# Modulation sections g1, sh2, sc2 and g2 of a hybrid mLSTM/attention block: from float32 products on TensorE to sums on GpSimd during attention

## The chip, the cores and the metric

The kernel runs on one core of one Trainium2 chip. The metric is the device time of one execution in microseconds (us). A profile is one more execution, recorded instruction by instruction; its times are counted from its first instruction. The engines are named PE (TensorE), DVE (VectorE), ACT (ScalarE), POOL (GpSimd) and SP (SyncE, which here issues most of the DMAs). PEld is TensorE's loading of weights.

## The reference, cut to what matters

```python
silu_c = jax.nn.silu(c)                               # [1, 1024]
mod = (silu_c @ w_mod[l] + b_mod[l])[:, None, :]      # [1024] @ [1024, 6144]
sh1, sc1, g1, sh2, sc2, g2 = jnp.split(mod, 6, axis=-1)
h = rmsnorm(x, norm1_g[l]) * (1.0 + sc1) + sh1
y, yc = token_mix(h, hc, w_in[l], ...)                # projections, mLSTM, attention, merge
x = x + g1 * y
x = x + g2 * swiglu(rmsnorm(x, norm2_g[l]) * (1.0 + sc2) + sh2, w_ffn_gate[l], w_ffn_up[l], w_ffn_down[l])
```

One layer, 1024 tokens, width 1024, a context of 256 tokens, 8 query heads and 2 key/value heads of 128 in attention. The modulation is a vector times a matrix of 1024 by 6144. Its first two sections (sh1, sc1) are wanted at once; the other four (g1, sh2, sc2, g2, each 1024 columns) only after attention.

## The kernel before, in words

All large products are float32 products by three TensorE products of halves (`mm3`: high by high, high by low, low by high; each operand is split by `split`, ACT writing the high half and DVE or POOL the low one, line 99). The order is: first modulation, norm, transposes; 25 units of projections; mLSTM heads; first half of the merge; attention; second half of the merge; output projection by halves of the tokens and quarters of the columns; feed-forward; down.

Big tiles of 4 KB a partition ("slots", tile name `s`) are given out and taken back in a ring; PSUM banks come from four tags (X, K, Y, Z). The program text sets what is computed; a scheduler behind it decides in which order the instructions stand on each engine, and each engine then works through its own list in that order, waiting on semaphores. SP's list of DMAs is in order too.

The four later sections are computed by `modulation_rest(ps, i)` in eight blocks of 512 columns, each called once between other stages: blocks 0 and 1 (g1) after projection units 14 and 15, blocks 4 to 7 (sh2, sc2) in the second half of the merge after column tiles 1, 2, 4 and 5, blocks 2 and 3 (g2) in the output projection after quarters 1 and 2. A block (`mod_block`, tile `macc`) loads four slots of 512 KB of w_mod and makes eight plain float32 products whose weights are the silu(c) columns, on four column tiles of TensorE side by side (line 300); DVE copies the four partial rows out of PSUM (line 304); then either one product with a selector sums them to a row (tile `mg`, line 344) which goes to DRAM with its bias, or four small ones sum them and put channels on partitions (tile `mch`, line 312).

Attention (`attention`, a generator) goes through 16 tiles: two key/value groups of eight tiles of 128 tokens, each tile four heads; a step is one head. A step makes scores of the next head (tile `sc`), transposes the probabilities of this one (tile `pt`), and makes a quarter of the product of probabilities and values of the tile before (`attn_values`, bank `av`, of which there is one). In the second quarter the inverse sums of rows (tile `dg`, set to zero by POOL at line 1100) are transposed and copied by DVE (tile `rrow`, line 1073), and POOL spreads them over all partitions by four `partition_broadcast` (tile `rs`, line 1076):

```python
            rows = pool.tile([P, P], F32, name="rrow", tag="rrow", bufs=1)
            nc.vector.tensor_copy(rows, rb[:, 0:P])
            self.rs = pool.tile([P, 512], F32, name="rs", tag="rs", bufs=1)
            for h in range(4):
                nc.gpsimd.partition_broadcast(self.rs[:, h * P:(h + 1) * P], rows[32 * h:32 * h + 1, :])
```

In the fourth quarter DVE multiplies `av` by `rs` into `yaf` (line 1080), which frees the bank. Besides these broadcasts POOL has in attention the zeroing of `dg` and, once, five low halves of the values of the second group (tile `vv`).

Of the kernel before, what the change touches and what calls it, by code (L numbers as in the profile page):

```python
# [17 lines left out]
P = 128  # L18
# [19 lines left out]
class Slots:  # L38
    """Tiles of 4 KB a partition, given out and taken back by hand."""
# [22 lines left out]
    def drop(self, pool):  # L62
        """Gives out no more tiles of a pool."""
        self.gone.append(pool)
        self.free = [x for x in self.free if x[0] is not pool]


class Carve:
    """Small tiles out of slots."""
# [18 lines left out]
class Block:  # L88
# [12 lines left out]
    def mm3(self, out, lhs, rhs, first, last):  # L101
        """out (+)= lhs^T rhs, with lhs and rhs as (hi, lo)."""
        nc = self.nc
        nc.tensor.matmul(out, lhsT=lhs[0], rhs=rhs[0], start=first, stop=False)  # L104
        nc.tensor.matmul(out, lhsT=lhs[0], rhs=rhs[1], start=False, stop=False)  # L105
        nc.tensor.matmul(out, lhsT=lhs[1], rhs=rhs[0], start=False, stop=last)  # L106

    def rstd(self, pool, ss, n, name):
        """(ss / n + eps) ** -0.5 for a small tile of sums of squares."""
# [14 lines left out]
    def load_s(self, slots, w, k0, nk, c0, n, scale=None, lo_eng=None):  # L124
        """Columns c0..c0+n of nk row blocks of w, as (hi, lo) slots [P, nk, n]."""
# [10 lines left out]
    # ------------------------------------------------------------------ constants  # L136
    def constants(self):
# [6 lines left out]
        # selectors over the four column tiles of the modulation products  # L144
# [3 lines left out]
        # additive masks of the two scan directions: key on partitions, query along the row  # L148
# [5 lines left out]
    def channel_params(self, ps):  # L154
        """Per-channel vectors, channel on partitions."""
# [19 lines left out]
        # silu of the conditioning vectors, one column per stream, padded to a column tile  # L175
# [8 lines left out]
    # ------------------------------------------------------------------ products by seven  # L184
    # C = A B by 2 x 2 blocks, A the transposed weights, B the rows by channel:
    #   P1 = A11 B11   P2 = A12 B21   P3 = S4 B22   P4 = A22 T4   P5 = S1 T1   P6 = S2 T2   P7 = S3 T3
    #   S1 = A21 + A22   S2 = S1 - A11   S3 = A11 - A21   S4 = A12 - S2
    #   T1 = B12 - B11   T2 = B22 - T1   T3 = B22 - B12   T4 = B21 - T2
    #   U2 = P1 + P6   U3 = U2 + P7   C11 = P1 + P2   C12 = U2 + P5 + P3   C21 = U3 + P4   C22 = U3 + P5
    RIGHT = {1: "11", 2: "21", 3: "22", 4: "4", 5: "1", 6: "2", 7: "3"}  # L190

    def grow(self, *names):
        """Room for two more channel blocks of each right operand."""
        for name in names:
            self.B.setdefault(name, []).append([self.slots.get([P, 2, 512], F32R) for i in range(2)])
# [9 lines left out]
    def t_stage(self, w, col):  # L205
        """A pair of column tiles of w, by halves of its rows."""
# [5 lines left out]
    def t_own(self, u):  # L212
        """A11 and A12."""
# [12 lines left out]
    def t_sums(self, u):  # L226
        """S1 over A21, S2 over A11, S4 over A12; S3 ready."""
# [13 lines left out]
    def t_rest(self, u, i):  # L241
        """S2 and S1, or S4 and A22."""
# [13 lines left out]
    def combine(self, n, o, c11, c12, c21, c22, early=False):  # L256
        """Takes product n into the blocks of C; early: product 4 comes before 6 and 7."""
# [26 lines left out]
    # ------------------------------------------------------------------ modulation  # L284
    def mod_block(self, ps, tag, cols):
        """Four column tiles of partial sums of (silu(c), silu(c_ctx)) @ w_mod at two runs of 256 columns."""
# [20 lines left out]
    def mod_channels(self, rows, ps, tag, n):  # L307
        """Sums the partial rows and puts channels on partitions: [P, 4, n]."""
# [7 lines left out]
    def modulation_first(self, ps, half):  # L316
        """Scale A1 and shift B1 of both streams for channel blocks 0, 1, 4, 5 or 2, 3, 6, 7."""
# [15 lines left out]
    def modulation_rest(self, ps, i):  # L333
        """Block i of 8: g1, g2 (rows to DRAM), sh2, sc2 (channels on partitions)."""
        nc = self.nc
        bm = self.ch("b_mod")
        j0, b = (2, 5, 3, 4)[i // 2], i % 2
        c0 = j0 * D + b * 512
        rows = self.mod_block(ps, "X", (c0, c0 + 256))
        if i < 4:  # L340
            row = self.slots.get([P, 1024], F32)
            nc.sync.dma_start(row[0:1, 0:512], self.io["b_mod"][0:1, c0:c0 + 512])
            o = ps("Y", "mg")
            nc.tensor.matmul(o[0:2, :], lhsT=self.sel, rhs=rows[:, 0], start=True, stop=True)
            nc.vector.tensor_tensor(row[0:1, 512:1024], o[0:1, :], row[0:1, 0:512], op=ALU.add)
            nc.sync.dma_start(self.d_g[i // 2:i // 2 + 1, b * 512:(b + 1) * 512], row[0:1, 512:1024])
            self.slots.put(rows, row)
            return
        m = self.mod_channels(rows, ps, "Y", 1)[:, :, 0]
        hs = slice(4 * b, 4 * b + 4)  # L350
        if j0 == 3:
            nc.vector.tensor_tensor(self.B2[:, hs], m, bm[:, 24 + 4 * b:28 + 4 * b], op=ALU.add)
        else:
            t = self.st.tile([P, 4], F32, name="modt2", tag="modt2", bufs=2)
            nc.vector.tensor_tensor(t, m, bm[:, 32 + 4 * b:36 + 4 * b], op=ALU.add)
            nc.vector.scalar_tensor_tensor(out=self.A2[:, hs], in0=t, scalar=1.0, in1=self.ch("norm2_g")[:, hs], op0=ALU.add, op1=ALU.mult)

    # ------------------------------------------------------------------ norm, transposes
# [10 lines left out]
    def first_norm(self, rows):  # L369
        """Rows of ctx and x over their norms."""  # L370
# [9 lines left out]
    def first_turn(self, k, fc):  # L380
        """h = xhat * A + B for channel block k, channels on partitions: lat, ctx."""
# [15 lines left out]
    def first_mods(self, q):  # L397
        """Channel blocks 0, 1, 4, 5 or 2, 3, 6, 7 of h, and the right operands from them."""
# [34 lines left out]
    # ------------------------------------------------------------------ gates  # L433
    def gate_loads(self):
        """Stationary operands: (hi, lo) columns for the high part of h, (hi, 0) for its low part."""
# [14 lines left out]
    def gates(self):  # L450
        """Gates of every token: G [P, NP, 16]."""
# [23 lines left out]
    # ------------------------------------------------------------------ projections  # L475
# [3 lines left out]
    def t_unit(self, kind, col, dst):  # L479
        """256 columns of h @ w_in, transposed: the load steps and the products."""  # L480
# [64 lines left out]
    def taps(self, out, z, ch, n):  # L545
        """Five taps along a row with zeros around it, bias and silu."""
# [24 lines left out]
    def tok_unit(self, kind, cols, dst):  # L571
        """Two runs of 256 columns of h @ w_in, tokens on partitions."""
# [99 lines left out]
    def rows_of(self, dst, t, m, c):  # L672
        """Columns c..c+256 of m token tiles."""
        return dst[t * P:(t + m) * P, c:c + 256].rearrange("(t p) c -> p t c", p=P)

    # ------------------------------------------------------------------ attention operands
    def attn_tables(self):
        """Rope tables and norm gains, the scale of the scores in that of q."""
# [8 lines left out]
    def head_norm(self, z, g, junk):  # L687
        """RMS norm of two heads of a few token tiles, in place."""
# [30 lines left out]
    # ------------------------------------------------------------------ mLSTM heads  # L719
    def head_load(self, h):  # L720
        """Operands of a head, as load steps."""
# [33 lines left out]
    def head(self, pool, h, X):  # L755
        """Steps of one head; heads take turns."""
        nc, slots, ps = self.nc, self.slots, self.ps
        # keys with tokens on partitions, and q k^T of every lat tile: both directions use it
# [72 lines left out]
        # norm over the head, gain, sigmoid(o), channels on partitions  # L831
# [21 lines left out]
    def merge_load(self, hp, n):  # L853
        """Four row blocks (two heads) of 256 columns of w_pa."""
        self.wpa[hp, n] = self.load_s(self.slots, self.io["w_pa"], 4 * hp, 4, n * 256, 256, lo_eng=self.nc.vector)

    def merge_unit(self, hp, n):
        """Columns n of sigmoid(zg_m) * (ym @ w_pa), transposed: the part of two heads."""
# [26 lines left out]
    def row_rstd(self, pool, xts, nm, junk):  # L885
        """rsqrt(mean x^2 + eps) of row tiles [P, D]."""
# [6 lines left out]
    # ------------------------------------------------------------------ gate scans  # L893
    def gate_scan(self, G):
        """Per token and (direction, head, tile): a = li - F, the weights of the state and of the
        state's update, exp(-m_t), and rows of -B for the products."""
# [17 lines left out]
        # rows: (head, tile) on partitions, tokens along the row  # L914
# [19 lines left out]
        # the end values of every (head, tile) on all partitions  # L934
# [22 lines left out]
        # back to tokens on partitions  # L957
# [25 lines left out]
        # rows of -B to DRAM, to be broadcast over partitions  # L983
# [7 lines left out]
    # ------------------------------------------------------------------ attention  # L991
# [20 lines left out]
    def attn_q(self, pool, ps, g, t):  # L1012
        """q of four heads of one kv group for a token tile, transposed and split."""
# [11 lines left out]
    def attn_scores(self, pool, ps, h, qt, kt):  # L1025
        """Scores of one head and the negated row maxima."""
# [11 lines left out]
    def attn_exp(self, pool, h, sc, st, dg):  # L1038
        """exp(s - max) of one head; the inverse row sums go to a column of dg."""
# [20 lines left out]
    def attn_values(self, pool, ps, g, t, PT, vv, dg, ya, part):  # L1060
        """A quarter of p^T v for four heads of a token tile; the last one scales by the inverse sums."""
# [21 lines left out]
    def attention(self, pool, ps):  # L1083
        """A generator: the first step readies the operands, the second the first scores, then
        it takes the pools of the products and runs to the end."""
# [24 lines left out]
        ptp, ya = yield  # L1110
# [730 lines left out]
```

## Time and profile before

| what | value |
|---|---|
| median of 3 runs | 2320.58 us (2313.97 to 2321.31) |
| span of the profiled execution | 2315.2 us, 31157 instructions |
| busy PE / PEld | 2175.2 us (94%) / 1797.7 us (78%) |
| busy DVE / ACT / POOL | 1590.1 us (69%) / 995.3 us (43%) / 763.8 us (33%) |
| mean granted TensorE clock | 0.975 |
| attention, first to last broadcast of `rs` | 1106.5 to 1386.4 us |

The page gives the profiled execution by its span, and no time around it; the median of the runs lies 5.4 us above that span. A busy share is an average over stages: in attention PE is busy throughout and POOL hardly at all. PE's clock is given as a share of full speed; where it stands near 0.5 the engine runs at the lower of its two levels (1.2 of 2.4 GHz).

### The profile page before, as it was taken

Reading aid. Unit: us, or ns where it says so; the run is one execution under the profiler, and the core shown is the slowest. Engines: PE = TensorE matmul, PEld = TensorE weight load, DVE = VectorE, ACT = ScalarE, POOL = GpSimd, SP = SyncE. Lnnn points to the kernel's source line nnn. Section 1 sums busy time; section 2 is a strip of 40 time slices with the busy share of each in tenths; the row PEclk is TensorE's granted clock in tenths of the full one; section 3 lists DMA queues with packets and bytes.
Section 4 is the critical chain, followed back from the end, with each engine's and each line's share of the span. In section 5 each row is a group of like instructions: output and inputs, shape, how many; then the busy total and the mean of one; then the engine's idle time right before and its main releaser. Section 6 shows DMA issues by size and latency. Waiting matters only on the chain. (4 is left out here: it accounts for less than half of the span.)

```text
span 2315.2 us, 31157 instructions
## 1 busy us (share of the span) xinstructions
PE 2175.2 (94%) x11387; PEld 1797.7 (78%) x11387; DVE 1590.1 (69%) x2855; ACT 995.3 (43%) x1997; POOL 763.8 (33%) x619
## 2 busy tenths in 40 slices
PE   5899999999999798999999998999899999999996
PEld 2698888978887686877888886789688888876875
DVE  5666576566879785876887873365846464678997
ACT  5434434243443564643777772134523232334332
POOL 2322232312323140311001004331554444457765
PEclk8999999999999899999999999999899999999999
DMA  7132232243233922046000016661143323265421
GB/s 259 55 93 100 92 101 96 92 141 128 84 101 107 307 70 97 10 144 220 15 22 21 15 42 218 220 225 57 46 132 96 109 94 111 96 218 179 159 91 73
DMA packets 179577, 262.43 MB, mean 113 GB/s; under 512 B 13136, under 2 KB 119640, under 8 KB 179424
## 3 DMA queue, kind: packets, MB, share of 16 engines
q1 hardware_dynamic: 169504, 236.62, 30.9%
q10 hardware_dynamic: 9920, 23.82, 2.6%
q8 instruction: 90, 1.47, 0.3%
q14 instruction: 63, 0.52, 0.1%
HBM read 190.10 MB, written 70.30 MB: 112 GB/s over the span
## 5 line engine op out<-in xcount | busy, mean ns | idle before, releaser
L98 ACT ACTIVATE s<-s 128x1024 fp32r<-128x1024 f32 (+2 forms) x446 | 369.2, 851 | 684.4 <-DVE s L233 74.5
L104 PE MATMUL pr<-s,s 128*128 128x512 f32 (+1 forms) x1736 | 624.7, 361 | 19.5 <-DVE s L261 9.9
L106 PE MATMUL pr<-s,s 128*128 128x512 f32 (+1 forms) x1736 | 623.9, 360 | 7.4 <-POOL s L99 4.5
L105 PE MATMUL pr<-s,s 128*128 128x512 f32 (+1 forms) x1736 | 624.1, 360 | 7.1 <-POOL s L99 5.1
L99 POOL TENSOR_TENSOR s<-s,s 128x1024 fp32r<-128x1024 f32 (+1 forms) x199 | 407.2, 2056 | 665.1 <-ACT s L98 488.0
L99 DVE TENSOR_TENSOR s<-s,s 128x1024 fp32r<-128x1024 f32 (+2 forms) x247 | 314.6, 1280 | 133.5 <-ACT s L98 107.1
L104 PEld LDWEIGHTS pr<-s,s 128*128 128x128 f32 x1736 | 331.2, 191 | 79.2 <-ACT s L98 13.4
L106 PEld LDWEIGHTS pr<-s,s 128*128 128x128 f32 x1736 | 329.6, 190 | 62.2 <-POOL s L99 6.7
L105 PEld LDWEIGHTS pr<-s,s 128*128 128x128 f32 x1736 | 330.2, 190 | 59.9 <-POOL s L99 6.2
L104 PE MATMUL pj<-s,s 128*128 128x512 f32 (+1 forms) x696 | 250.9, 361 | 17.9 <-DVE s L1740 13.8
L105 PE MATMUL pj<-s,s 128*128 128x512 f32 (+1 forms) x696 | 248.9, 358 | 7.3 <-POOL s L99 7.3
L106 PE MATMUL pj<-s,s 128*128 128x512 f32 (+1 forms) x696 | 248.1, 356 | 1.1 <-POOL s L99 1.1
L261 DVE TENSOR_TENSOR s<-s,pr 128x512 f32<-128x512 f32 x200 | 133.1, 680 | 83.5 <-PE pr L106 78.9
L1530 DVE TENSOR_TENSOR s<-s,pr 128x512 f32<-128x512 f32 x154 | 100.1, 678 | 111.9 <-PE pr L106 55.5
L104 PEld LDWEIGHTS pj<-s,s 128*128 128x128 f32 x696 | 133.8, 192 | 49.4 <-DVE s L1740 17.9
L105 PEld LDWEIGHTS pj<-s,s 128*128 128x128 f32 x696 | 133.7, 192 | 26.2 <-POOL s L99 7.7
L106 PEld LDWEIGHTS pj<-s,s 128*128 128x128 f32 x696 | 133.7, 192 | 21.6 <-POOL s L99 1.7
L1058 DVE TENSOR_TENSOR PT<-pt,PT 128x512 fp32r<-128x512 f32 (+1 forms) x192 | 112.5, 598 | 35.0 <-ACT PT L1057 32.9
L1043 ACT ACTIVATE pr<-sc,st 128x512 f32<-128x512 f32 (+1 forms) x192 | 118.0, 622 | 33.4 <-DVE st L1035 32.9
L1540 POOL TENSOR_TENSOR s<-s,s 128x512 f32<-128x512 f32 x44 | 67.8, 1542 | 168.1 <-ACT s L98 81.8
L1057 ACT ACTIVATE PT<-pt 128x512 fp32r<-128x512 f32 (+1 forms) x192 | 94.5, 525 | 56.1 <-PE pt L1054 56.0
L1033 DVE TENSOR_REDUCE st<-sc 128x1 f32<-128x512 f32 (+1 forms) x192 | 109.4, 589 | 0.8 <-PE sc L106 0.8
(313 smaller groups left out, 3522.4 us busy)
## 6 DMA issues: line engine op xcount, KB each, us to landing
s<-in_w_in_dram SPq DMA_DIRECT2D x60, 512.0 KB, 3.8
d_act<-s SPq DMA_DIRECT2D x74, 256.0 KB, 2.1
s<-d_act SPq DMA_DIRECT2D x37, 512.0 KB, 5.3
s<-in_w_mod_dram SPq DMA_DIRECT2D x32, 512.0 KB, 6.0
s<-in_w_ffn_gate_dram SPq DMA_DIRECT2D x22, 512.0 KB, 4.3
s<-in_w_ffn_up_dram SPq DMA_DIRECT2D x22, 512.0 KB, 3.8
s<-in_w_ffn_down_dram SPq DMA_DIRECT2D x22, 512.0 KB, 5.1
s<-in_w_mod_dram SPq DMA_DIRECT2D x32, 256.0 KB, 5.1
```

Of the source, the lines that this page charges most:

```text
L98: nc.scalar.activation(hi, src, AF.Copy)
L99: (lo_eng or nc.gpsimd).tensor_tensor(lo, src, hi.bitcast(F32), op=ALU.subtract)
L104: nc.tensor.matmul(out, lhsT=lhs[0], rhs=rhs[0], start=first, stop=False)
L105: nc.tensor.matmul(out, lhsT=lhs[0], rhs=rhs[1], start=False, stop=False)
L106: nc.tensor.matmul(out, lhsT=lhs[1], rhs=rhs[0], start=False, stop=last)
L261: eng.tensor_tensor(out, a, b, op=ALU.add)
L1033: nc.vector.tensor_reduce(st[:, j:j + 1], o[:, 0:n], axis=AX.X, op=ALU.max)
L1043: nc.scalar.activation(pr[:, s0:s0 + n], sc[j][:, 0:n], AF.Exp, bias=st[:, 3:4], accum_out=st[:, 4 + j:5 + j])
L1057: nc.scalar.activation(hi, src, AF.Copy)
L1058: nc.vector.tensor_tensor(lo, src, hi.bitcast(F32), op=ALU.subtract)
L1530: nc.vector.tensor_tensor(out, a, b, op=ALU.add)
L1540: nc.gpsimd.tensor_tensor(g, g, o, op=ALU.mult)
```

## The change

`modulation_rest` becomes a generator that attention drives with one `next` after each step. It goes through the sections g1, sh2, sc2, g2, and in each through eight row blocks of w_mod: a load of 512 KB by SP (tile `wm`, two buffers), on POOL a multiplication of the 128 by 1024 block by the silu(c) column (`tensor_scalar`) and an addition into an accumulator (`tensor_tensor`), which starts as zeros with the bias in one row. Then TensorE sums the accumulator over partitions with a tile of ones: two products of 512 columns for g1 and g2, eight products of one column for sh2 and sc2. The eight calls elsewhere go, and with them 64 float32 products, their loads and the copies out of PSUM. (Comments and blank lines that the diff also removes are left out here.)

```diff
-    def modulation_rest(self, ps, i):
-        nc = self.nc
-        bm = self.ch("b_mod")
-        j0, b = (2, 5, 3, 4)[i // 2], i % 2
-        c0 = j0 * D + b * 512
-        rows = self.mod_block(ps, "X", (c0, c0 + 256))
...
+    def modulation_rest(self, pool):
+        nc, slots, ps = self.nc, self.slots, self.ps
+        sections = (2, 3, 4, 5)
+        seq = [(j0, k) for j0 in sections for k in range(KT)]
+        loaded, accs = [], {}
+        def load():
...
+            j0, k = seq[i]
+            w = pool.tile([P, D], F32, name="wm", tag="wm", bufs=2)
+            nc.sync.dma_start(w, self.io["w_mod"][k * P:(k + 1) * P, j0 * D:(j0 + 1) * D])
+            loaded.append(w)
+        def start(j0):
+            accs[j0] = slots.get([P, D], F32)
+            nc.gpsimd.memset(accs[j0], 0.0)
+            nc.sync.dma_start(accs[j0][0:1, :], self.io["b_mod"][0:1, j0 * D:(j0 + 1) * D])
+        start(sections[0])
+        load()
+        for i, (j0, k) in enumerate(seq):
+            load()
+            if k == 2 and j0 != sections[-1]:
+                start(j0 + 1)
+            acc = accs[j0]
+            nc.gpsimd.tensor_scalar(loaded[i], loaded[i], self.sc[:, k, 0:1], None, op0=ALU.mult)
+            nc.gpsimd.tensor_tensor(acc, acc, loaded[i], op=ALU.add)
+            yield
+            if k + 1 < KT:
+                continue
+            if j0 in (2, 5):
+                for b in range(2):
+                    o = ps("Y", "mg")
+                    nc.tensor.matmul(o[0:2, :], lhsT=self.ones[:, 0:2], rhs=acc[:, b * 512:(b + 1) * 512], start=True, stop=True)
+                    nc.vector.tensor_copy(acc[0:1, b * 512:(b + 1) * 512], o[0:1, :])
+                nc.sync.dma_start(self.d_g[j0 // 5:j0 // 5 + 1, :], acc[0:1, :])
+            else:
+                m = ps("Y", "mch")
+                for j in range(KT):
+                    nc.tensor.matmul(m[:, j:j + 1], lhsT=acc[:, j * P:(j + 1) * P], rhs=self.ones[:, 0:1], start=True, stop=True)
...
+            slots.put(accs.pop(j0))
+            yield
@@ attention
-        ptp, ya = yield
+        ptp, ya, side = yield
...
             pr = nxt() if nxt else None
+            next(side, None)
@@ run
-            if i in (14, 15):
-                self.modulation_rest(PS, i - 14)
...
-        attn.send((pt, yaf))
+        wm, close_wm = pool("wm")
+        attn.send((pt, yaf, self.modulation_rest(wm)))
+        close_wm()
...
-            if n in (1, 2, 4, 5):
-                self.modulation_rest(PS, 3 + n if n < 3 else 2 + n)
...
-            if not half and u in (1, 2):
-                self.modulation_rest(PS, 1 + u)
```

How the lists of the engines move is seen at two places. First POOL's list in attention, before, at the first two tiles (`ISA` without operands is a pair of instructions that sets POOL up for another set of functions, in the profile MODIFY_POOL_CONFIG; `ISA rs<-rrow` is the broadcast):

```order
L1100 MEMSET dg 128x128
L1076 ISA
L1076 ISA rs<-rrow 128x128 x4
L1100 MEMSET dg 128x128
L1076 ISA rs<-rrow 128x128 x4
```

POOL's list after the change, from the end of the second tile into the third (line numbers are those of the changed file: 352 zeroes an accumulator, 362 multiplies, 363 adds, 1102 is the broadcast):

```order
L363 TENSOR_TENSOR s_9831<-s_9831,wm 128x1024
L1102 ISA
L1102 ISA rs<-rrow 128x128 x4
L362 ISA
L362 TENSOR_SCALAR wm<-wm,sc 128x1024
L352 MEMSET s_10373 128x1024
L363 TENSOR_TENSOR s_9831<-s_9831,wm 128x1024
L362 TENSOR_SCALAR wm<-wm,sc 128x1024
L1102 ISA
L1102 ISA rs<-rrow 128x128
L363 ISA
L363 TENSOR_TENSOR s_9831<-s_9831,wm 128x1024
```

Between one broadcast and the next there now stand multiplications and additions, and an `ISA` on either side of each broadcast group; in some tiles the four broadcasts are parted as well. In attention the list before has this `ISA` twice ahead of broadcasts and twice ahead of additions; the list after has it 20 times ahead of broadcasts and 20 times ahead of multiplications or additions; of the latter the last, behind the last broadcast, is in either list.

Second, PE's list in the second half of the merge, before, between column tiles 1 and 2 (`pj` is the merge's bank):

```order
L106 MATMUL pj<-s_13410,s_9716 128x512
L300 MATMUL macc<-s_13607,sc 32x512 x2
L300 MATMUL macc<-s_13611,sc 32x512 x2
L300 MATMUL macc<-s_13615,sc 32x512 x2
L300 MATMUL macc<-s_13619,sc 32x512 x2
L104 MATMUL pj<-s_13396,s_13467 128x512
```

and the same place after the change:

```order
L106 MATMUL pj<-s_13538,s_9666 128x512
L104 MATMUL pj<-s_13524,s_13595 128x512
L105 MATMUL pj<-s_13525,s_13595 128x512
L106 MATMUL pj<-s_13524,s_13596 128x512
L104 MATMUL pj<-s_13524,s_13595 128x512
```

The eight products of the block are gone, and the next column tile follows at once.

## Rows read from the trace of the kernel before

**Rows 1.** The page, part 1: busy us, share of the span, instructions of each engine.

```profile
PE 2175.2 (94%) x11387; PEld 1797.7 (78%) x11387; DVE 1590.1 (69%) x2855; ACT 995.3 (43%) x1997; POOL 763.8 (33%) x619
```

**Rows 2.** Stretches of 40 us: length, busy us by engine, PEclk, DMA share, GB/s.

```profile
1200.00:1240.00 40.00, 40.00 (x237) 32.59 (x237) 32.18 (x83) 28.94 (x80) 4.18 (x14) 1.00 0.04 14
```

**Rows 3.** Timeline of PE: start us, busy us, line, operation, count; summing products of two blocks.

```profile
541.75 1.02 PE L344 MATMUL mg<-s,sel 128*2 128x512 f32 x2
...
1417.62 1.92 PE L300 MATMUL macc<-s,sc 128*32 128x512 f32 x16
...
1420.52 0.98 PE L312 MATMUL mch<-sel,s 128*128 128x1 f32 x8
```

**Rows 4.** Timeline, PE at three blocks; in brackets PE's idle time before and its releaser.

```profile
511.33 1.32 PE L300 MATMUL macc<-s,sc 128*32 128x512 f32 x8 [3.44 <-DMA s<-in_w_mod_dram]
...
1478.02 1.87 PE L312 MATMUL mch<-sel,s 128*128 128x1 f32 x8 [3.98 <-DVE s L304]
...
1532.06 1.38 PE L344 MATMUL mg<-s,sel 128*2 128x512 f32 x2 [2.17 <-DVE s L304]
```

**Rows 5.** Stretches of 10 us around these waits, columns as in rows 2.

```profile
500.00:510.00 10.00, 7.89 (x35) 6.13 (x33) 9.93 (x12) 5.14 (x6) 2.41 (x1) 1.00 0.83 241
510.00:520.00 10.00, 8.67 (x30) 2.82 (x30) 4.26 (x6) 2.40 (x4) 1.28 (x1) 0.83 0.69 275
...
1480.00:1490.00 10.00, 10.00 (x35) 8.01 (x36) 2.67 (x5) 1.57 (x2) 0.65 (x2) 0.76 0.71 262
...
1530.00:1540.00 10.00, 7.94 (x48) 6.72 (x49) 4.46 (x6) 2.52 (x4) 2.37 (x1) 0.83 0.83 292
```

**Rows 6.** POOL by line, 1079 to 1399: count, busy us, mean ns, idle before.

```profile
L1076 POOL PARTITION_BROADCAST rs<-rrow x64 | 20.3, 424 | 46.3 <-DVE rrow L1073 33.9 <-issue 5.9 <-DVE qt L1022 5.9
...
L99 POOL TENSOR_TENSOR s<-s,s 128x1024 fp32r<-128x1024 f32 x2 | 4.7, 2372 | 41.5 <-ACT s L98 41.5
L99 POOL TENSOR_TENSOR vv<-vr,vv 128x256 fp32r<-128x256 f32 x5 | 3.6, 732 | 12.0 <-ACT vv L98 11.9
```

**Rows 7.** POOL by line and shape, whole span, columns as in rows 6.

```profile
L799 POOL TENSOR_TENSOR qw<-s,wq 128x128 f32<-128x128 f32 x128 | 59.8, 488 | 133.7 <-PE num L807 98.1 <-ACT s L819 18.9 <-ACT sw L802 7.6
...
L783 POOL MEMSET C<- 128x516 f32 x8 | 4.1, 527 | 12.5 <-PE num L807 6.9 <-PE pr L106 5.5
...
L152 POOL TENSOR_SCALAR_AFFINE_SELECT mask<-mask 128x128 f32<-128x128 f32 x1 | 0.3, 293 | 0.0
```

**Rows 8.** Timeline of POOL at the broadcasts of tiles 0 and 8.

```profile
1088.64 2.39 POOL L99 TENSOR_TENSOR s<-s,s 128x1024 fp32r<-128x1024 f32 x1 [6.58 <-ACT s L98]
1100.34 0.21 POOL L1100 MEMSET dg<- 128x128 f32 x1 [9.32 <-PE pt L1071]
1106.48 1.29 POOL L1076 PARTITION_BROADCAST rs<-rrow  x4 [5.93 <-issue]
...
1255.64 0.20 POOL L1100 MEMSET dg<- 128x128 f32 x1 [2.52 <-PE pt L1071]
1261.74 1.29 POOL L1076 PARTITION_BROADCAST rs<-rrow  x4 [5.90 <-DVE qt L1022]
```

**Rows 9.** Line 1076, its set-ups: duration ns min/median/max, first and last start us.

```profile
L1076 POOLq MODIFY_POOL_CONFIG  x4: 11/11/11, 1100.5 to 1256.1; - x4
```

**Rows 10.** Line 99 on POOL, 1385 to 1400, its set-ups, columns as in rows 9.

```profile
L99 POOLq MODIFY_POOL_CONFIG  x2: 134/134/134, 1386.3 to 1386.3; - x2
```

**Rows 11.** Timeline, end of attention: ACT, POOL and PE.

```profile
1383.83 4.29 ACT L98 ACTIVATE s<-yaf 128x512 fp32r<-128x512 f32 x8 [1.15 <-PE av L106]
...
1385.10 1.26 POOL L1076 PARTITION_BROADCAST rs<-rrow  x4 [13.65 <-DVE rrow L1073]
...
1393.72 6.04 POOL L99 TENSOR_TENSOR s<-yaf,s 128x512 fp32r<-128x512 f32 x4 [7.36 <-DVE s L99]
1396.11 0.79 PE L105 MATMUL pj<-s,s 128*128 128x512 f32 x1 [7.30 <-POOL s L99]
```

**Rows 12.** The page, part 6: a DMA issue, count, KB each, median us to landing.

```profile
s<-in_w_mod_dram SPq DMA_DIRECT2D x32, 512.0 KB, 6.0
```

More of the change, by code (lines that the diff above doesn't have):

```diff
@@ L331, in modulation_first @@
                     nc.vector.scalar_tensor_tensor(out=self.A1[:, s, k:k + 2], in0=t, scalar=1.0, in1=g1[:, k:k + 2], op0=ALU.add, op1=ALU.mult)
-    def modulation_rest(self, ps, i):
-        nc = self.nc
-        bm = self.ch("b_mod")
-        j0, b = (2, 5, 3, 4)[i // 2], i % 2
-        c0 = j0 * D + b * 512
-        rows = self.mod_block(ps, "X", (c0, c0 + 256))
[L340 to L356, printed above, removed]
@@ new lines, in modulation_rest @@
+    def modulation_rest(self, pool):
[4 more added lines that the diff above has]
+        def load():
+            i = len(loaded)
+            if i >= len(seq):
+                return
+            j0, k = seq[i]
[28 more added lines that the diff above has]
+                    nc.tensor.matmul(m[:, j:j + 1], lhsT=acc[:, j * P:(j + 1) * P], rhs=self.ones[:, 0:1], start=True, stop=True)
+                if j0 == 3:
+                    nc.vector.tensor_copy(self.B2, m[:, 0:KT])
+                else:
+                    nc.vector.scalar_tensor_tensor(out=self.A2, in0=m[:, 0:KT], scalar=1.0, in1=self.ch("norm2_g")[:, 0:KT], op0=ALU.add, op1=ALU.mult)
+            slots.put(accs.pop(j0))
+            yield
```

## Prediction

> **What bounds the kernel now.** The page's first part comes first: PE is busy 94% of the span, POOL 33% [rows 1]. That is a mean over stages, so the second view is the stretches, and of them attention, since the work goes there: in 40 us PE is busy 40.0, DVE and ACT about 30, POOL 4.2, and the DMA engines 4% [rows 2]. Read by that row alone, POOL and DMA have all the room that the change needs. The third view is POOL's timeline there, because a share of busy time doesn't show what an engine waits for: ahead of the broadcasts of tile 0 POOL stands idle for 5.93 us and ahead of those of tile 8 for 5.90 [rows 8]. At both places, and at no other broadcast, it has just been set up for another set of functions [rows 9]; the first has the releaser "issue", that is, nothing that the profile shows was still awaited. The reader is to see a price that isn't in the busy time at all. The way back has one too: after the last broadcast (1385.10 + 1.26 = 1386.36) comes the other set-up [rows 10], and the next addition starts at 1393.72, 7.36 us later; the ACT work that makes its operand had ended at 1383.83 + 4.29 = 1388.12 [rows 11]. The DVE instruction named as releaser makes another tile. PE waits 7.30 us for that addition [rows 11].
>
> **What goes.** Eight blocks of eight products. One block holds PE for 1.92 us, and PE was in a gapless row of products there [rows 3]: 8 x 1.92 = 15.4 us. At three of the blocks PE also waits: 3.44 us for a load of w_mod, 3.98 and 2.17 us for DVE's copy of the partial rows [rows 4], together 9.6 us. After each wait PE is granted less clock: 0.83, 0.76 and 0.83 over 10 us [rows 5], so 1.7 + 2.4 + 1.7 = 5.8 us. The summing products stay in number: four `mg` at 1.02 us and sixteen `mch`, four in 0.98 us [rows 3], together 4 x 1.02 + 4 x 0.98 = 8.0 us; they move into attention, and by the next part PE has nothing to do there for much longer than that, so their old place is a gain too. Sum 38.8 us. Bounds: 23.4 if each wait comes back for another operand (ahead of the first of them DVE was busy 9.93 of 10 us [rows 5], so it can), and 38.8. I take 35.
>
> **What comes, on POOL.** 32 additions of 128 x 1024, 2.37 us each [rows 6]. 32 multiplications of one operand by a column: the trace has none. Zeroing costs 0.20 us at 128 columns [rows 8] and 0.53 at 516 [rows 7], 0.83 ns a column, so 0.95 us at 1024, and that is the lower bound, since it reads nothing; the addition with its two operands, 2.37, is the upper one. At 128 columns the one-operand form that the trace has, the affine select, takes 0.293 us between 0.204 and 0.488 [rows 7, 8], 0.31 of the way; 0.31 of the way from 0.95 to 2.37 is 1.4, which I take. The page "GPSIMD Engine Reference" of the Trainium skill (section Engine selection) puts one-input operations at roughly line rate, which with its clock would be an estimated 0.85 us; no run here shows it, and the sum would be 14 us lower.
>
> The list of POOL settles the rest. It starts with six pairs of these, then the broadcasts of tile 0; in the tiles 1 to 8 stand the other 26, and around every group of broadcasts the two set-ups. From the end of tile 0's broadcasts to the start of tile 8's, in microseconds: 26 additions 61.6, 26 multiplications 36.4, two zeroed accumulators 1.9, eight zeroed `dg` 1.6, the broadcasts of seven tiles at 1.29 [rows 8] 9.0, five `vv` at 0.73 [rows 6] 3.7, 19 set-ups for broadcasts at 5.9 us 112.1, and 19 back at 7.36 us 139.8. Sum 366. Before, that stretch is 1107.8 to 1261.7, 153.9 us [rows 8], so tile 8 is 212 us later. Ahead of tile 0 the six pairs and two zeroings are 24.5 us of new work against idle times of 6.58 and 9.32 [rows 8]: 9 us more. That makes 221.
>
> None of it is hidden. What is queued behind POOL's work is the next group of broadcasts; for `rs` waits DVE's multiplication into `yaf`, DVE's list is in order, and `av` has one bank, so PE can't begin the next tile's values. PE's cover is one tile: between tile 8 and the last broadcast lie seven tiles in 1385.10 - 1261.74 = 123.4 us [rows 8, 11], 17.6 each, while POOL now needs 366/8 = 46 a tile. The loads are no bound: 512 KB land in 6.0 us [rows 12] and two buffers allow two loads in that time plus a pair of operations, 9.8 us, against two pairs with their set-ups, some 23 to 46. SP's list holds `qr` loads behind loads that wait for POOL, but each of them behind an addition that stands before the broadcasts which PE needs earlier. From tile 9 on there is nothing of the change in POOL's list, and the seven tiles take their 123 us as before.
>
> The price of a set-up is the step with most weight, and the reason against the change. The same page (section Instruction dispatch) says that the first call after loading another function library pays about 6 us that no instruction of the profile shows. The trace agrees on the way there (5.93, 5.90) and pays again at the second time; back it shows 7.36. By the page both ways would cost 5.95, and the sum would be 26 us lower.
>
> **Sum.** Against the profiled execution: 2315.2 - 35 + 221 = 2501 us. The median of the runs is 5.4 us above that span, so 2507.
>
> **Rivals.** (a) The way back costs nothing of its own, and the 7.36 us at the end of attention were something else. For it: one clean instance only; in the other, POOL's next operand came from ACT anyway. Against it: everything that I can see awaited was there 5.6 us before. Price: 139.8 us less, 2367.
> (b) PE's part adds to POOL's. Between the broadcasts of one tile and the first of the next PE has to go from `yaf` to the next transposed `dg`, and POOL's own work in that gap is as short as 7.4 + 2 x 1.4 + 0.95 + 2.4 + 5.9 = 19.4 us. At most one tile of PE's work, 17.6 us, lies between, so at full clock it fits. A PE that waits 25 us a tile is granted less, as after the waits before [rows 5]; at half the clock it is up to 35 us, 15 more than the gap, in eight tiles up to 125. The multiplication at 2.37 us would add 31. I put this case at 2550 to 2640, with 2575 in its middle.
> (c) The other side: faster. If set-ups cost nothing when they alternate, a tile holds four pairs and one group, 4 x 3.77 + 1.3 + 0.2 = 16.6 us, less than its 17.6 to 19, and everything is hidden; the summing products cost PE again, so the gain is 35 - 8 = 27: 2294. It is decided at about 1 us for both set-ups together: there are 19 pairs of them in eight tiles, 2.4 a tile, and a tile has some 2 us to spare. Against it stand 5.93, 5.90 and 7.36; for it only the 4.2 us of 40.
>
> **Chances.** The forecast, 2430 to 2550, has 0.62; (b) 0.20; (a) 0.12; (c) 0.05; 0.01 for a balance near no change. Predicted 2507. The bounds: below, 38 set-ups at 5.9 (28 less), multiplications at 0.95 (14 less) and the full 38.8 us of gain (4 less) make 2461, and a way back at 4 us instead makes 2430; above, 2.37 for the multiplication makes 2538, and half of (b)'s 125 us 2570, nearly all of it 2610. The range 2425 to 2610 leaves out (a), (c) and the end of (b), together under 0.2. A difference of 0.3% (7 us) is about what a measurement of this kernel tells from none: faster 0.05, same 0.01, slower 0.94.
>
> **What would show it.** Right: attention from about 1075 to 1600 us; 20 set-ups each way (each a pair of records), each followed by 5.9 to 7.4 us without work on POOL; DVE waiting at `yaf` for POOL; PE busy under half in that stretch, at a lower granted clock; no `macc` after 120 us, and the second half of the merge and the output projection some 20 to 25 us shorter. From tile 9 on steps as before. Wrong: broadcasts that start within a microsecond of a set-up; POOL idle ahead of `rrow` instead (then PE is the pace, case b); multiplications far from 1.4 us; a merge no shorter than before.

## Result, and the profile after

The changed kernel takes 2563.08 us (median of 4 runs, 2561.06 to 2565.15) against 2320.94 us for the kernel before in the same comparison: a ratio of 1.1052, 95% interval 1.1032 to 1.1072, slower by a tenth. The forecast was 2507 in a range of 2425 to 2610. The profiled execution has a span of 2559.3 us, 244.1 more than before, against a forecast of 2501.

First the page, part 1 (busy us, share, instructions), against [rows 1]:

```profile
PE 2196.5 (86%) x11259; PEld 1816.7 (71%) x11259; DVE 1589.9 (62%) x2843; ACT 995.8 (39%) x1995; POOL 932.9 (36%) x687
```

POOL is busy for only 169 us more, and stands at 36%. Nobody would find the loss in this row. The stretch from the end of tile 0's broadcasts to the start of tile 8's shows it (length, busy us by engine, clock, DMA share, GB/s):

```profile
1110.57:1529.64 419.07, 198.82 (x930) 151.77 (x931) 130.64 (x324) 112.44 (x304) 152.00 (x96) 0.71 0.12 37
```

It took 154.0 us before [rows 8] and takes 419.1 now. No engine is busy for half of it, PE's granted clock falls to 0.71, and the DMA engines are busy for 12% of it. What is it waiting for? POOL's timeline in the middle of it (start, busy, line, operation; in brackets the idle time before it and its releaser):

```profile
1346.70 0.43 POOL L1102 PARTITION_BROADCAST rs<-rrow  x1 [6.55 <-issue]
1354.82 5.69 POOL L362 TENSOR_SCALAR wm<-wm,sc 128x1024 f32<-128x1024 f32 x2 [7.69 <-issue]
1360.48 2.33 POOL L363 TENSOR_TENSOR s<-s,wm 128x1024 f32<-128x1024 f32 x1
1369.36 0.43 POOL L1102 PARTITION_BROADCAST rs<-rrow  x1 [6.55 <-issue]
1377.20 2.33 POOL L363 TENSOR_TENSOR s<-s,wm 128x1024 f32<-128x1024 f32 x1 [7.41 <-issue]
1386.02 0.74 POOL L1102 PARTITION_BROADCAST rs<-rrow  x2 [6.49 <-issue]
1393.78 2.85 POOL L362 TENSOR_SCALAR wm<-wm,sc 128x1024 f32<-128x1024 f32 x1 [7.03 <-issue]
```

This is one tile's group of four broadcasts. It spans 40 us, of which the broadcasts themselves are 1.6. At every change between a broadcast and a sum, in either direction, POOL is idle for 6.5 to 7.7 us with the releaser "issue": nothing that the profile knows of was awaited. In these 40 us no engine but POOL does anything (length, busy us of PE, PEld, DVE, ACT and POOL, clock, DMA share, GB/s):

```profile
1346.70:1386.76 40.06, 0.00 (x0) 0.00 (x0) 0.00 (x0) 0.00 (x0) 11.92 (x8) 0.50 0.09 26
```

The set-ups themselves appear by line (duration ns, first and last start us), each of the 20 there and 20 back as a pair of records that is itself nearly free:

```profile
L1102 POOLq MODIFY_POOL_CONFIG  x40: 1/1/17, 1102.2 to 1523.9; - x40
...
L362 POOLq MODIFY_POOL_CONFIG  x24: 129/134/134, 1110.5 to 1498.8; - x24
...
L363 POOLq MODIFY_POOL_CONFIG  x10: 129/129/129, 1165.5 to 1369.7; - x10
```

Lines 362 and 363 have 34 of the records of the way back, 17 pairs; of the other three pairs two stand ahead of `vv` and one behind the last broadcast of attention. The whole stretch on POOL, by line and shape (count, busy us, mean ns, idle before by releaser), to be held against [rows 6]:

```profile
L362 POOL TENSOR_SCALAR wm<-wm,sc 128x1024 f32<-128x1024 f32 x26 | 74.0, 2847 | 87.8 <-issue 86.5 <-DMA wm<-in_w_mod_dram 1.3
L363 POOL TENSOR_TENSOR s<-s,wm 128x1024 f32<-128x1024 f32 x26 | 61.1, 2350 | 35.8 <-issue 35.3
L1102 POOL PARTITION_BROADCAST rs<-rrow x29 | 11.1, 429 | 121.6 <-issue 89.6 <-DVE st L1059 13.7 <-DVE st L1061 12.4
L99 POOL TENSOR_TENSOR vv<-vr,vv 128x256 fp32r<-128x256 f32 x5 | 3.5, 715 | 14.0 <-issue 14.0
L352 POOL MEMSET s<- 128x1024 f32 x2 | 1.9, 946 | 0.0
L1126 POOL MEMSET dg<- 128x128 f32 x8 | 1.6, 201 | 7.8 <-PE pt L1097 7.8
```

So the set-ups to broadcasts cost 121.6 us (19, 6.40 each) and those back 86.5 + 35.3 + 14.0 = 135.8 us (19, 7.15 each): 257.4 us, more than the 244 by which the span grew. Five of the 19 on the way there, 32 of the 121.6 us, name a DVE instruction as releaser instead of "issue"; it makes another tile, and in each of the five `rrow` had been there for 5.9 us or more, so they are counted as set-ups too. Waits for other engines or for data are 7.8 + 1.3 + 0.5 = 9.6 us in 419. POOL waits for hardly anybody, so POOL's list is the pace. Who waits for POOL, in the waits of 1110 to 1530 (who, for what: us, times, longest):

```profile
DVE yaf L1106 <- POOL rs L1102: 136.2, 7, 44.9
...
PE mch L376 <- POOL s L363: 100.1, 2, 54.2
...
PE av L104 <- DVE yaf L1106: 77.4, 3, 46.4
...
DVE dg L1071 <- POOL dg L1126: 37.7, 3, 14.3
```

Three kinds: `yaf` for its broadcast, as forecast; PE's summing products `mch` for the sum that is still growing; and DVE for the zeroing of `dg`, a 0.2 us instruction that stands in POOL's list behind 1024-column work. The last two were not in the prediction.

### The profile page after: what moved, and what is told of

It reads as the page before. It is cut to its first block, busy times and chain, and to the rows that moved or that the text cites. A ratio compares the mean times of both kernels' runs of the same rounds, so it can differ in the third digit from the quotient of the medians.

```text
span 2559.3 us, 31010 instructions
## 1 busy us (share of the span) xinstructions
PE 2196.5 (86%) x11259; PEld 1816.7 (71%) x11259; DVE 1589.9 (62%) x2843; ACT 995.8 (39%) x1995; POOL 932.9 (36%) x687
## 5 line engine op out<-in xcount | busy, mean ns | idle before, releaser
L104 PE MATMUL av<-PT,vv 128*128 128x512 f32 x160 | 71.1, 444 | 77.6 <-DVE yaf L1106 77.4
```

## The experiments

The theories. **1**: the changes of function set on POOL, 13.55 us a round trip (6.40 there and 7.15 back), are the pace. **2**: the sums fill POOL, whatever the set-ups do. **3**: PE's list is held by summing products that wait for POOL. **4** came later: small POOL instructions placed in a list full of sums.

**Set-ups alone, in the kernel before (e7, e8, e4).** A POOL instruction of 128 x 8 that computes nothing of use is added to every tile, behind the four broadcasts (e7), between them (e8), or both (e4).

```diff
...
             for h in range(4):
                 nc.gpsimd.partition_broadcast(self.rs[:, h * P:(h + 1) * P], rows[32 * h:32 * h + 1, :])
+                if h == 1:                                   # e8, e4
+                    v = self.rs[:, 128:136]
+                    nc.gpsimd.tensor_tensor(self.rs[:, 256:264], v, v, op=ALU.mult)
+                if h == 3:                                   # e7, e4 (e4 reads columns 256 and 384)
+                    nc.gpsimd.tensor_tensor(self.jk, self.rs[:, 384:392], self.rs[:, 384:392], op=ALU.mult)
```

Expected of e7: 

> The kernel before, with one multiplication of 128 x 8 on POOL behind the four broadcasts of every tile, which computes nothing of use: one set-up each way a tile, 13.55 + 1.3 + 0.4 = 15.2 us on POOL of the 18.7 that a tile has. Theory 1 with the cover as the prediction has it: hidden, since rs may come 8.7 us after rrow and the set-up ahead of it takes 6.4: 2315 to 2330. If a set-up costs whatever stands beside it: 16 x 13.55 = 217 more, 2532; if half of it: 2420.

Expected of e8: 

> The same with the small multiplication between the broadcasts of a tile instead of behind them, 15 set-ups each way too, the same POOL time a tile. Theory 1: the set-ups now lie between rrow and rs, where 8.7 us are free: 13.55 + 1.6 - 8.7 = 6.5 us a tile late, 16 x 6.5 = 104, 2419 (2370 to 2450). If only POOL's sum a tile counts (15.2 of 18.7): 2321, as e7.

Expected of e4: 

> The kernel before, with two multiplications of 128 x 8 on POOL in each tile, one between the broadcasts and one behind them, that compute nothing of use; no other work is added. They make two set-ups each way a tile. Theory 1: 2 x 13.55 + 1.3 + 0.2 + 0.2 = 28.8 us a tile on POOL against 18.7, 16 x 10.1 = 162 more, 2483 (2430 to 2530). Theory 2 (sums, not set-ups): 2321.

Measured, one run each: e7 2328.32 (before 2322.22 there, so no difference that can be told), e8 2362.59 (40 more), e4 2547.55 (233 more than 2314.98). The arithmetic is 0.2 us each time; what differs is where the set-ups stand and how many a tile has, one each way or two. POOL's timeline of e7:

```profile
1141.33 0.19 POOL L1080 TENSOR_TENSOR jk<-rs 128x8 f32<-128x8 f32 x1 [7.13 <-issue]
1145.74 0.21 POOL L1104 MEMSET dg<- 128x128 f32 x1 [4.22 <-PE pt L1072]
1151.87 1.29 POOL L1077 PARTITION_BROADCAST rs<-rrow  x4 [5.93 <-DVE qt L1023]
1160.25 0.19 POOL L1080 TENSOR_TENSOR jk<-rs 128x8 f32<-128x8 f32 x1 [7.08 <-issue]
```

and of e8:

```profile
1160.42 0.98 POOL L1076 PARTITION_BROADCAST rs<-rrow  x3 [0.23 <-DVE rrow L1073]
1168.20 0.20 POOL L1079 TENSOR_TENSOR rs<-rs 128x8 f32<-128x8 f32 x1 [6.79 <-issue]
1174.27 0.43 POOL L1076 PARTITION_BROADCAST rs<-rrow  x1 [5.88 <-issue]
```

The prices are those of the changed kernel, around an instruction of 0.2 us: they belong to the change of function set and not to the large sums. In e7 POOL still waits some 4 us for PE in a tile (4.22 in the row above), so one round trip fits. In e8 it lies between `rrow` and the last broadcast, and `yaf` starts 14.9 us after `rrow` (tile 3; 9.0 before). Yet an ordinary tile hardly pays for that: from tile 0's `yaf` to tile 7's it takes 136.7 us in e8, 135.4 in e7 and 135.2 before. Stretches of e8, from `yaf` to `yaf`, tiles 0 to 7 and then 7 to 8 (columns as above):

```profile
1119.64:1256.33 136.69, 134.28 (x766) 109.95 (x766) 106.81 (x268) 92.29 (x254) 12.45 (x41) 1.00 0.06 17
1256.33:1301.35 45.02, 28.13 (x134) 19.90 (x132) 21.20 (x53) 20.41 (x56) 5.60 (x12) 0.84 0.05 15
```

In the first PE is busy for all but 2.4 us. Most of the 40 us is lost in the second, 45.0 us for the 19.9 that it takes before: there the `vv` of the second group come between the broadcasts as well, and three round trips stand in one tile. The last tile, behind which PE has no other tile, takes 5.9 us longer (15.6 for 9.7). So the expectation was missed because it charged 6.5 us to every tile; what decides is how many round trips one tile holds, and not where its only one stands. In e4 there are two in every tile, and they exceed it. The loss went beyond the 162 us of POOL's sum because POOL waits as well: 37.1 us for `rrow` ahead of broadcasts of four tiles, 29.6 for PE ahead of the zeroing of `dg`, 18.1 for ACT ahead of `vv`. There the parts of POOL and PE do add, which is the prediction's rival (b) in small.

**The change without set-ups (e1), and its control (e12).** `rs` is spread by two DMAs, to DRAM and back to all partitions, instead of the broadcasts, in the changed kernel (e1) and in the kernel before (e12).

```diff
-            for h in range(4):
-                nc.gpsimd.partition_broadcast(self.rs[:, h * P:(h + 1) * P], rows[32 * h:32 * h + 1, :])
+            d = self.d_rs[8 * g + t]
+            nc.sync.dma_start(d, rows.rearrange("(h q) j -> h q j", h=4)[:, 0, :])
+            nc.sync.dma_start(self.rs.rearrange("p (h j) -> p h j", h=4), d.partition_broadcast(P))
```

Expected of e1: 

> The changed kernel, but rs is spread by two DMAs (four rows of 128 to DRAM, read back to all partitions) in place of the four partition_broadcasts, so no set-up stands in attention; all loads, multiplications and additions of the change stay. Theory 1 (set-ups on POOL pace attention): the 38 gaps of 257.5 us between tile 0 and tile 8 go; POOL needs 4 x (2.85 + 2.35) + 0.2 = 21.0 us a tile in eight tiles against the 18.7 that a tile takes before, so at most 8 x 2.3 = 18 us stay, less the gain of 24 to 35: 2285 to 2325, middle 2305. Theory 2 (the sums themselves fill POOL and pace attention): most of the loss stays, 2450 or more. Theory 3 (PE's list stands behind the summing products, which wait for POOL): up to 115 us of PE's waits stay, about 2400. Unknown: the time of the two DMAs; it is hidden up to 8.7 us, the distance from rrow to yaf before.

Expected of e12: 

> The kernel before with nothing changed but the way of rs: two DMAs instead of four broadcasts by POOL. It separates what e1 and e11 owe to the missing set-ups from what the DMAs themselves do. Theory: before has only two set-ups each way in attention, the DMAs are hidden by the 8.7 us between rrow and yaf, and only the last tile has no cover: 2310 to 2325. If the DMA way were a gain by itself, 2300 or less, and e11 would owe its gain to it; if it cost something in every tile, 2330 or more, and e1 would understate what the set-ups cost.

Measured: e1 2347.77, ratio 1.0137 (1.0117 to 1.0157) to before; e12 2315.23, ratio 0.9982 (0.9966 to 0.9998). The DMAs by themselves are worth 0.2% (0.3% at the end of the interval), so of the 242 us that the change lost, about 215 go with the broadcasts, all sums staying. e1 takes two things away at once: the set-ups, and the place of `rs` in POOL's list behind the sums. That it is mainly the set-ups is told by the 257.4 us counted above, by e4, where they cost 233 us without any sum, and by e3 below. That is theory 1, and theory 2 falls as the main cause. No run puts the four broadcasts of a tile together beside the sums, with one round trip a tile; how much of the loss that alone would take away stays open. But e1 lies above its range, 56 us over the gain alone (e2). That rest became a question of its own, below.

**The gain alone (e2).** The changed kernel with the generator's loads, multiplications and additions left out.

Expected of e2: 

> The changed kernel without the loads of wm, the multiplications and the additions: the four sections hold only their biases, so the output lacks the matrix part of g1, sh2, sc2 and g2. What is left is the removal of the eight blocks and the summing products in attention. The prediction's term: 35 less 8 for the summing products in a PE that is busy throughout, 2294; bounds 23.4 - 8 and 38.8 - 8, so 2290 to 2306. Rival (PE's gaps between stages come back for other reasons, and the removed blocks were free): 2315 to 2321.

Measured: 2291.85, ratio 0.9891 (0.9875 to 0.9908), 23.1 us faster than 2314.98. That is what the removed blocks are worth with the summing products in attention paid for; the forecast of this part was 27.

**The summing products a tile later (e3).** Theory 3 had 100 us of waits at `mch` for it.

```diff
-            if k == 2 and j0 != sections[-1]:
+            if k == 4 and j0 != sections[-1]:
                 start(j0 + 1)
...
+            if k == 3 and j0 != 2:
+                total(j0 - 1)      # the products of the section before, unchanged
+                yield
```

The next accumulator is started two blocks later, when the late products have given theirs back.

Expected of e3: 

> The changed kernel with the summing products of each section put one tile later, when POOL has long finished that section, so PE does not stand behind a sum that is still growing. POOL's list then has 24 set-ups each way in place of 20. Theory 1 (POOL's list is the pace): PE's 115 us of waits at mch and mg go elsewhere, and four round trips of 13.55 us come on top, 2563 + 54 = 2617 (2600 to 2635). Theory 3 (PE's list): 2563 + 54 - 115 = 2502, or less.

Measured: 2615.29, one run, 52 more than the changed kernel, where four more round trips at 13.55 us make 54. PE's waits in 1100 to 1600:

```profile
PE av L104 <- DVE yaf L1110: 133.8, 6, 54.2
...
PE mch L366 <- POOL s L380: 24.8, 2, 19.5
```

The waits at `mch` fell from 100.1 to 24.8, and three quarters of that came back at `av`, 133.8 for 77.4. Theory 3 falls: PE waits for POOL's list, and where in its own list it does so is of no account while POOL is the pace.

**What was left in e1 (e5, e6, e9, e10, e11).** In e1 DVE waits for the DMA of `rs`, and SP's list shows why (start of the issues, time they span):

```profile
1148.76 26.52 SPq L347 DMA_DIRECT2D wm<-in_w_mod_dram  x6
1175.38 0.50 SPq L1102 DMA_DIRECT2D d_rs<-rrow  x1
1175.97 0.39 SPq L1042 DMA_DIRECT2D qr<-d_q  x1
1178.54 0.32 SPq L1103 DMA_DIRECT2D rs<-d_rs  x1
```

Six loads stand ahead of it, each held until POOL frees a buffer. So in e5 GpSimd issues the loads itself (`nc.gpsimd.dma_start`), and e6 spreads the sums over all 16 tiles as well (`if i % 9 < 5: next(side, None)`).

Expected of e5: 

> The kernel of e1, with the loads of wm issued by GpSimd instead of SP. In e1 DVE waited 59.4 us at yaf for the DMA of rs, five times, and in SP's list up to six loads of wm, each waiting for a buffer that POOL frees, stand ahead of that DMA. If that list is what is left (theory 1 with SP's list as the second cause), those waits go: POOL has 21 us a tile in eight tiles, but nothing of PE's waits for it except the summing products, 2292 (gain alone) to 2310. If POOL's sums themselves are what is left (theory 2 for the rest), it stays at 2348 within 8 us. Issuing on POOL has a cost of its own that no row shows; 32 loads at 1 us would still be hidden.

Expected of e6: 

> The kernel of e5 with the 36 steps of the sums spread over all 16 tiles (five steps of every nine heads), so POOL has 11.9 us a tile of 18.7. If nothing but POOL's lead and SP's list stood against the change, it comes to the gain alone, 2292 (2286 to 2300), a version faster than both kernels. If the sums cost PE something else (DMA traffic, DVE beside POOL), 2305 or more.

Measured: e5 2356.40, ratio 1.0149 (1.0130 to 1.0167); e6 2360.90, ratio 1.0172 (1.0153 to 1.0190). Both expectations missed: neither is better than e1. The waits of e5 in 1090 to 1250 name the next link:

```profile
DVE dg L1071 <- POOL dg L1127: 32.9, 3, 13.2
...
PE mg L370 <- POOL s L363: 9.2, 1, 9.2
...
DVE yaf L1107 <- DMA rs<-d_rs: 4.8, 2, 4.3
```

`yaf` hardly waits any more, as intended, but the wait has moved to the zeroing of `dg` (in e6 too: 39.6 us, four times, in attention). That it stands in POOL's list behind several pairs is theory 4. In e9 two tiles `dg` are zeroed once by DVE; e10 does that with the loads back on SP.

```diff
-                dgs[g, t] = pool.tile([P, P], F32, name="dg", tag="dg", bufs=2)
-                nc.gpsimd.memset(dgs[g, t], 0.0)
+                dgs[g, t] = dg2[t % 2]
...
```

Expected of e9: 

> The kernel of e5, with two tiles dg set to zero once by DVE instead of one a tile by POOL (only columns 0, 32, 64 and 96 are written afterwards). In e5 DVE waits at dg for that POOL instruction, three times, 32.9 us, because it stands in POOL's list behind several pairs of sums; then no step of a tile needs POOL. Theory 4 (what is left of the loss is the place of small POOL instructions in a list full of sums): the gain alone, 2292, plus what the sums of the end still hold up: up to 10 us at mg as in e5, and vv of the second group behind all 32 pairs, about 20 us: 2292 to 2320, middle 2305. If the sums cost PE in another way (DMA traffic, DVE and POOL side by side), it stays near e5, 2345 or more.

Expected of e10: 

> The kernel of e1 (loads of wm by SP) with dg set to zero once. Against e9 it tells what SP's list is worth: the DMA of rs stands in it behind up to six loads that wait for POOL's buffers. Theory: both links held, so cutting one of them alone leaves most of e1's 2348: 2325 to 2348. If dg was the only link, it equals e9; if SP's list never mattered, too.

Measured: e9 2339.14, ratio 1.0096 (1.0075 to 1.0116); e10 2348.49, ratio 1.0132 (1.0112 to 1.0151). With SP's list in the way, freeing `dg` is worth nothing (e10 is e1); with both cut it is worth a part, less than expected of e9. The largest wait left in e9 is one of DVE at `yaf`, 27.7 us long, and it leads to POOL a third time; PE also waits 9.8 us at `mg` for a sum. POOL's timeline of e9:

```profile
1217.36 0.94 POOL L352 MEMSET s<- 128x1024 f32 x1
```

and SP's:

```profile
1218.33 0.25 SPq L353 DMA_DIRECT2D s<-in_b_mod_dram  x1
1218.68 0.51 SPq L1102 DMA_DIRECT2D d_rs<-rrow  x1
1220.31 0.33 SPq L1103 DMA_DIRECT2D rs<-d_rs  x1
```

The zeroing of the next accumulator stands in POOL's list among the sums; the load of its bias on SP waits for it; the DMAs of `rs` are queued behind that load. SP had been silent for 47 us (its issue before is at 1170.77), and `rrow` had been there since 1187.3. e11 takes e9, starts an accumulator only when the section before it is half done, puts the summing products late as in e3, and spreads the sums (`if i % 7 < 4`).

Expected of e11: 

> The kernel of e9 with the summing products a tile late (as e3) and the sums spread over the 16 tiles (four steps of every seven heads), so that POOL has finished a section before PE's list comes to its sum, and vv of the second group stands ahead of the last section. If the theory is complete, the gain alone: 2292 (2286 to 2300), faster than the kernel before. With a further cause 2305 or more.

Measured: 2296.84, ratio 0.9913 (0.9897 to 0.9928), 0.9% faster than the kernel before, and 5 us above the gain alone. The stretch 1110 to 1280 of e11:

```profile
1110.00:1280.00 170.00, 168.17 (x977) 137.29 (x976) 133.82 (x339) 117.28 (x324) 138.19 (x76) 1.00 0.35 105
```

Here POOL is busy for 138 of 170 us beside a PE that is busy for 168 at full clock (132.03 at 0.88 in e1 and 169.65 at full clock in e2, where there are no sums). So the sums with their DMA traffic cost PE next to nothing by running beside it; e11 changes three things at once, and which of them cut the last wait was not tried apart.

## Why the prediction was right, and where it was off

Right in the sign, the cause and the count: 19 set-ups each way between tiles 0 and 8, each charged. The terms of that stretch, forecast and measured:

| term | forecast us | measured us |
|---|---|---|
| 26 additions | 61.6 | 61.1 |
| 26 multiplications | 36.4 | 74.0 |
| 19 set-ups for broadcasts | 112.1 | 121.6 |
| 19 set-ups back | 139.8 | 135.8 |
| broadcasts, zeroing, `vv` | 16.2 | 18.1 |
| other waits | 0 | 9.6 |
| the stretch | 366 | 419.1 |

(The measured terms sum to 420.2; neighbouring instructions overlap a little. The kernel before took 154.0 in this stretch.)

- **What comes, the multiplications**: the mis-sized term. I put them between zeroing (0.95) and addition (2.37) and took 1.4; they take 2.85, above the upper bound. The step that failed is "the addition with its two operands is the upper one", and with it the interpolation from a 128-column affine select. It is 37.6 of the 58 us by which the span exceeded the forecast. By the prediction's own list, "multiplications far from 1.4 us" was a sign of being wrong, and that sign did show. The Trainium skill, "GPSIMD Engine Reference", section Engine selection, has one-input operations at about line rate, an estimated 0.85 us here by its clock; the trace disagrees by more than three times, and the trace decides.
- **The set-ups**: right. The way there is 6.40 on average against 5.9 from two instances, the way back 7.15 against 7.36 from one; the two errors cancel in part (+9.5, -4.0). The same page (section Instruction dispatch) has about 6 us for the first call after a library is loaded: the trace agrees on the way there, and shows that the way back is charged too. Rival (a), a free way back, is excluded by the 19 rows, and e7 and e8 show that charge around an instruction of 0.2 us.
- **None of it is hidden**: right, for this list, with its 2.4 round trips a tile. e7 and e8 show the condition: one round trip in an ordinary tile is hidden, two are not (e4). PE's cover was put a little low: from `yaf` to `yaf` an ordinary tile takes 19.0 us before, while the 17.6 has the set-up ahead of tile 8 and the short last tile in its mean.
- **What goes**: from tile 8's broadcasts to the end the kernel takes 2315.2 - 1261.7 = 1053.5 us before and 2559.3 - 1529.6 = 1029.7 after, 23.8 less. Of that 2.7 lie in attention itself (1529.64 to 1650.31, 120.7 us to the last tile's broadcasts for 123.4 before), and 21.1 behind it, which is what was put down for the merge and the output projection (20 to 25). Ahead of tile 0 it is 2.8 us later (1109.28 for 1106.48), where the forecast had 9 less the gain of the first two blocks. Together 21 us of gain against 26.
- **Rival (b)**, PE's part on top of POOL's: 9.6 us of waits, nearly nothing here, though the clock did fall to 0.71; it shows in e4. The time landed where (b) begins (2550), for another reason: mainly the multiplication.
- **Rival (c)**, set-ups that cost nothing, was priced wrongly. It was to give 2294 with 16.6 us a tile on POOL; with 2.85 us for a multiplication that is 22.4, and e1, which has no set-ups, takes 2348. POOL's time a tile was not the only condition either: zeroing of `dg`, zeroing of an accumulator and SP's list each had to be taken out of POOL's way (e9, e11).
- **What would show it**: DVE waits at `yaf` (136.2 us), PE is busy under half (198.8 of 419.1), the last `macc` starts at 58.4 us, and from tile 8's broadcasts to those of the last tile the steps are nearly as before (120.7 us for 123.4). The summing products were costed at 8 us of PE's time and never as a wait; they held PE for 100 us, at no cost as e3 shows, but only because POOL was later anyway.
- **Luck**: the sign and the cause were not luck. That the time lies in the stated range is in part: it lies above the 2430 to 2550 of the forecast itself, among the times of rival (b), whose mechanism is nearly absent here.

## What to carry to other kernels

On GpSimd count the changes between custom functions and plain arithmetic in the engine's list, not the instructions: here one round trip took 13.55 us of POOL's time and none of it is in the busy share; one in a tile of 19 us was hidden, two or more were not. A lightly loaded engine is free only if nothing on the critical path stands behind the new work in its list, and the lists of the DMA queues that wait for it count as well: look for the 0.2 us instruction behind sums of some 5 us. When a wait is cut and the time stays, read the waits again before dropping the theory; here it took three links.

## What was not expected of the hardware

- A multiplication of 128 x 1024 by a column takes 2.85 us on POOL (26 in the stretch, mean 2847 ns), an addition of two such tiles 2.35: fewer operands, more time.
- The way back doesn't get cheaper with the instruction behind it: 7.2 and 7.1 us on average (6.8 to 7.6) ahead of a 128 x 8 product in e7 and e8, 7.15 in the changed kernel. The way there takes 6.0 and 5.9 us on average in e7 and e8 and 6.40 in the changed kernel; why is open. In e8 the way there takes 5.88 us although `rrow` had been there for 14 us.
- A load of 512 KB issued by GpSimd itself keeps POOL busy for 0.53 to 0.75 us, median 0.60 (32 loads each in e5 and e9).
